# Rows of a 290-column operand at a pitch of 304 floats on 64-byte boundaries, and half of a normalization moved behind the second unit product

## The chip, the cores and the metric

The kernel runs as one program on one core of a Trainium2 chip. The metric is the device time of one execution in microseconds, a median over runs. Besides the runs, one execution was taken with the hardware profiler; every span, wait and duration below comes from that one.

## The reference

One step of one layer of a streaming encoder, for 512 prompt frames and 64 sample frames of width 2048, all in float32. The layer is an adaLN-modulated RMSNorm, an input projection, two recurrences (gated linear attention, 4 heads; gated delta rule, 8 heads), an output projection with a gated residual, then a second normalization and a convolutional feed-forward block of width 5632. The change lies in that second half:

```python
h = rmsnorm(x, norm2[l]) * (1 + sc2) + sh2
f, s_f = conv_ffn(h, ffn_s[l], w_up[l], ffn_conv_w[l], ffn_conv_b[l], w_down[l])
x = x + g2 * f

def conv_ffn(h, st, w_up, ffn_conv_w, ffn_conv_b, w_down):
    gate, val = jnp.split(h @ w_up, 2, axis=-1)
    gate_c, new_st = causal_dwconv(gate, st, ffn_conv_w)
    act = jax.nn.silu(gate_c + ffn_conv_b) * val
    return act @ w_down, new_st
```

## The kernel before

Activations lie transposed: features on the 128 partitions, frames along the row. The 576 frames are two halves of 288 columns (256 prompt, 32 sample frames). Every float32 product is made of three fp32r products: each operand is split into a rounded `hi` (ScalarE, `Copy`) and the rest `lo` (VectorE, subtraction), and TensorE adds `wh*hi`, `wh*lo` and `wl*hi` in PSUM. One matmul is 128 x 128 weights on 288 or 290 columns; TensorE issues a weight load and a matmul for each.

The stages, in order of time: the head with norm and modulation; the input projection (`gemm`, `mm6`, L534 and L536) with the recurrences' small work placed between its matmuls as jobs, and the rest of the modulation streamed through VectorE (L794); the first half of the output projection from 1100 us on; its second half with the second normalization begun tile by tile (`norm_tile`, `pair_early`, `pair_begin`); `up`, the feed-forward's first product; `down` and `final`.

A slot (`slot`) is an SBUF tile `[128, 2, w]`, w = 290 unless 288 is asked for. The residual stream's tiles `x1[m]` are slots (two rows: the two halves). So are the operands of `up`, where row 0 holds `hi` and row 1 `lo`. Two columns per half (256 and 257) carry the shift vectors through the product, which makes 290 of 288.

`up` multiplies by a 7-product scheme on 2 x 2 blocks (Strassen, in Winograd's form). For each of 44 column tiles t there are products c = 0 to 6 (`up_product`): 8 pairs j, three matmuls each (L1335 `wh, hi`; L1336 `wh, lo`; L1337 `wl, hi`), 24 of 290 columns. The right operands are the combinations B11, T1, T2, B21, T3, B22, T4, kept in slots for all t. For pairs 4 to 7 most of them are made during t = 0 (`pair_late`). `up_prep` splits the weights two products ahead. The sums gather in three PSUM banks of a pool of four (`bank`), x for c = 0 and 3, z for 1 and 5, y for 2, 4 and 6. `up_out` combines them.

The normalization's scale enters only behind the products, as a row `rb` (1/rms of each frame, on all partitions; first used in `up_out` for c = 3, L1355). `norm_tile` sums the squares into `sqa`, stores the tile to memory (`xd`, L1166) and scales it (L1168, L1169). `norm_end`, called behind the first product of t = 0, does the rest: ten small matmuls sum over the partitions (L1248), VectorE (L1250) and GpSimd (L1251) make rsqrt, VectorE spreads it to diagonals `dg` (L1253), two fp32 products with ones broadcast these (L1259, two passes each), ScalarE copies them over `sqa` (L1260), and GpSimd sets four entries to one (L1261).

A tile framework records the program and orders each engine's instructions by priorities and its own estimates of when they become ready; an engine then runs its instructions strictly in that order. Buffers are reused as soon as their last reader is done, so a buffer's size and place also decide what waits for what. DMAs are issued from SyncE's queue, a few from ScalarE's; none from GpSimd. 16 KB of every partition, from address 0, are set aside as scratch for dynamic DMA descriptors unless the program asks otherwise.

Of the kernel before, what the change touches and what calls it, by code (L numbers as in the profile page):

```python
# [8 lines left out]
F32 = mybir.dt.float32  # L9
# [7 lines left out]
P = 128  # L17
# [7 lines left out]


HZ, ZS = 290, 258
X_AT = (1, 2, 3, 4, 5)

AHEAD, JOB_AHEAD = 80, 80  # L30
# [67 lines left out]
class Kern:  # L98
# [530 lines left out]
    def head(self, pool):  # L629
# [16 lines left out]
        places = [f"h{c}{k}" for k in range(15, 4, -1) for c in "hl"]  # L646
        slot = lambda: self.hslot(places.pop(0), [P, 512])
        junk = slot()

        def x_block(b):  # L650
            n = P if b < 4 else TS
            xt = [slot() for _ in range(4)]
            for q in range(4):
                f = slice(q * 512, (q + 1) * 512)
                nc.sync.dma_start(xt[q][:n], i["x_prompt"][0, b * P:(b + 1) * P, f] if b < 4 else i["x_sample"][0, :, f])
            ms4 = pool.tile([P, 8], F32, tag="ms4", bufs=2, name=self.name("ms4"))
            for q in range(4):
                A.activation(junk[:n], xt[q][:n], AF.Square, scale=float(D) ** -0.5, accum_out=ms4[:n, q:q + 1])
            V.tensor_reduce(ms4[:n, 4:5], ms4[:n, 0:4], axis=mybir.AxisListType.X, op=ALU.add)
            self.rsqrt(ms4[:, 5:6], ms4[:, 4:5], 1, n)  # L660
            for q in range(4):
                V.tensor_scalar_mul(xt[q][:n], xt[q][:n], ms4[:n, 5:6])
            per = 4 if b < 4 else 8
            for k0 in range(0, KD, per):
                ps = self.pgt()[:, 0]
                for k in range(k0, k0 + per):
                    T.transpose(ps[:, (k - k0) * n:(k - k0 + 1) * n], xt[k // 4][:n, k % 4 * P:(k % 4 + 1) * P],
                                self.c["ident"][:n, :n])
                if b < 4:
                    A.activation(xT[:, k0:k0 + per, b // 2, (b % 2) * P:(b % 2 + 1) * P],  # L670
                                 ps.rearrange("p (k t) -> p k t", k=per), AF.Copy)
                else:
                    for h in range(2):
                        A.activation(xT[:, k0:k0 + per, h, HP:HT],
                                     ps.rearrange("p (k h t) -> p k h t", k=per, h=2)[:, :, h], AF.Copy)
# [5 lines left out]
        def modulation(g):  # L681
            for mi in (1, 0):
                ps = self.bank()
                c0 = mi * D + g * 512
                for k0 in range(0, KD, 4):
                    yield
                    raws = [hraw().rearrange("p (k n) -> p k n", k=2) for _ in range(2)]
                    for n, raw in enumerate(raws):
                        k1 = k0 + 2 * n
                        nc.sync.dma_start(raw, i["w_ada"][0, k1 * P:(k1 + 2) * P, c0:c0 + 512].rearrange("(k p) n -> p k n", p=P))  # L690

                    for k in (2, 3, 0, 1):
                        with self.tc.issue_after(last) if k == 0 else nullcontext():
                            T.matmul(ps[32 * k:32 * k + 32], cs[:, k0 + k], raws[k // 2][:, k % 2], start=(k0 == 0), stop=(k0 == KD - 4))  # L694
                        last = nc.cur_bb.bb.instructions[-1]
                rw = pool.tile([P, 512], F32, tag="rw", bufs=1, name=self.name("rw"))
                V.tensor_copy(rw, ps)
                pc = self.transpose4(rw.rearrange("p (b t) -> p b t", b=4))
                m = pool.tile([P, 4, 2], F32, tag="msum", bufs=2, name=self.name("msum"))
                V.tensor_reduce(m, pc.rearrange("p b (j q) -> p b q j", j=4)[:, :, 0:2], axis=mybir.AxisListType.X, op=ALU.add)  # L700
                self.put_mod(mi, 4 * g, m)
                for _ in vectors:
                    pass
            self.scale_mod(s1, 1, "norm1", 4 * g)

        for n, _ in enumerate(modulation(0)):
            if n in X_AT:
                x_block(X_AT.index(n))

# [432 lines left out]

    def slot(self, place, dt, w=HZ):
        pool, tag = place
        return pool.tile([P, 2, w], dt, tag=tag, name=self.name("slot"))

# [1 line left out]
    def norm_begin(self):  # L1150
        self.s2 = self.cp.tile([P, KD, 2], F32, name="s2")
        self.scale_mod(self.s2, 4, "norm2", 0, KD)
        self.sq = self.sp.tile([P, 2, HZ], F32, tag="sqa", bufs=1, name="sqa")
        self.combos = {}

    def norm_tile(self, m, first):
# [83 lines left out]
    def norm_end(self):  # L1240

        nc = self.nc
        V, A, T = nc.vector, nc.scalar, nc.tensor
        w = HZ // 5 * 2
        av = self.sq.rearrange("p h t -> p (h t)")
        ps = self.bank()
        for b in range(5):
            T.matmul(ps[:w, b:b + 1], av[:, b * w:(b + 1) * w], self.c["ones"][:, 0:1], start=True, stop=True)  # L1248
        rs = self.small(8)
        V.tensor_scalar(rs[:w, :5], ps[:w, :5], 1.0 / D, EPS, op0=ALU.mult, op1=ALU.add)  # L1250
        nc.gpsimd.tensor_tensor(rs[:w, :5], rs[:w, :5], self.mhalf[:w, :5], op=ALU.pow)  # L1251
        dg = self.ub.tile([P, 5, w], F32, tag="ca", name=self.name("dg"))
        V.tensor_tensor(dg[:w], self.c["ident"][:w, :w].unsqueeze(1).to_broadcast([w, 5, w]),  # L1253
                        rs[:w, :5].unsqueeze(2).to_broadcast([w, 5, w]), op=ALU.mult)
        rb = self.rb = self.sq
        dv = dg.rearrange("p b t -> p (b t)")
        for h in range(2):
            ps = self.bank()
            T.matmul(ps[:, :HZ], self.c["ones"][:w], dv[:w, h * HZ:(h + 1) * HZ], start=True, stop=True)  # L1259
            A.activation(rb[:, h], ps[:, :HZ], AF.Copy)  # L1260
        nc.gpsimd.memset(rb[:, :, HP:ZS], 1.0)  # L1261
# [138 lines left out]
    def up(self):  # L1400
        self.fs = self.cp.tile([P, 2, 2, NFF], F32, name="fs")
        self.cb = self.ub.tile([P, 2 * HZ], F32, tag="cb", name="cb")
        self.nc.gpsimd.tensor_copy(self.cb[:, 0:2], self.zero3[:, :2])
        self.up_state(0)
        self.t2s = {}
        ahead = 2
        steps = [(t, c) for t in range(NFF) for c in range(7)]
        for n, (t, c) in enumerate(steps):
            if t == 0:
                for l in ((1,), (2,), (3,), (4,), (5, 6), (), ())[c]:  # L1410
                    for j in range(N_EARLY, NPAIR):
                        self.pair_late(l, j)
            if n + ahead < len(steps):
                self.up_prep(*steps[n + ahead])
            self.up_product(t, c)
            if n == 0:
                self.norm_end()

            if t > 0 and c == 0:
                with self.tc.issue_after(self.split_of):  # L1420
                    self.up_conv(t - 1, self.ca)
                self.up_state(t)
            if t > 0 and c == 2:
                with self.tc.issue_after(self.split_of):
                    self.up_act(t - 1, self.v, self.ca)
            self.up_out(t, c)
        self.up_conv(t, self.ca)
        self.up_act(t, self.v, self.ca)
# [308 lines left out]
```

## Time and profile before

| | |
|---|---|
| median of 3 runs | 2957.4 us (2954.98 to 2959.34) |
| the profiled execution: span from first to last instruction | 2955.2 us |
| its own time beside the span | not recorded apart; the span stands 2.2 us under the median |
| mean granted TensorE clock | 0.982 |
| busy: TensorE, VectorE, ScalarE, GpSimd | 96%, 70%, 40%, 11% |
| unit products of `up` | 1364.7 to 2367.1 us |

Rows of groups read: line, engine, operation, output<-inputs, shapes, count, then busy time in us and the mean of one in ns. That mean is the life of one matmul in the pipeline; a new one starts about every 133 ns, so three are in flight. Rows of the timeline read: start, length, engine, line, and in brackets how long the engine was idle before and what released it. The granted clock (PEclk) is the share of full speed that the throttle lets TensorE have.

### The profile page before, as it was taken

The numbers are of one execution on the slowest core, as the hardware profiler recorded it, in microseconds if no ns is written. First come the engines' busy times: TensorE is split into PE (matmuls) and PEld (weight loads), VectorE is DVE, ScalarE is ACT, GpSimd is POOL, SyncE is SP. The second block draws the span as 40 slices with busy tenths as digits, with TensorE's granted clock in tenths as the row PEclk, the third lists the DMA queues.
The fourth block names the chain that finished last, engine by engine and source line by source line (L and its number), as shares of the span: only waits on it lengthen the run. The fifth ranks groups of instructions, "written<-read, shape, count | busy, mean of one in ns | idle before, by whom it ended". The sixth has DMA issues, their size and how long they took to land.

```text
span 2955.2 us, 52052 instructions
## 1 busy us (share of the span) xinstructions
PE 2836.7 (96%) x20964; PEld 2744.9 (93%) x20964; DVE 2055.8 (70%) x3299; ACT 1180.8 (40%) x2029; POOL 325.7 (11%) x513
## 2 busy tenths in 40 slices
PE   6998999999899999999999999999999999999998
PEld 3688988999889998999999999999999999999997
DVE  2357777776568877367888888888888855555455
ACT  4235444444454433255444444444444421212123
POOL 0004223332300000000111111111111100000000
PEclk8999999999999999999999999999999999999999
DMA  8864545444454547642433333333333463333221
GB/s 260 285 194 134 169 137 146 142 143 140 138 148 126 157 125 214 172 128 82 117 105 105 105 110 105 105 109 111 100 105 114 145 219 99 115 102 111 86 80 65
DMA packets 535444, 395.53 MB, mean 134 GB/s; under 512 B 59657, under 2 KB 465412, under 8 KB 535204
## 3 DMA queue, kind: packets, MB, share of 16 engines
q1 hardware_dynamic: 527860, 390.54, 44.2%
q8 instruction: 165, 2.70, 0.4%
q10 hardware_dynamic: 7344, 1.67, 0.3%
q14 instruction: 75, 0.61, 0.1%
HBM read 356.47 MB, written 35.67 MB: 133 GB/s over the span
## 4 chain that ended last, share of the span: by engine, by line
PE 80%; DVE 6%; DMA 5%; POOL 4%; ACT 3%; issue 2%; SPq 0%; ACTq 0%; POOLq 0%; DVEq 0%
PE g L534 25%; PE g L536 13%; PE bank L1336 11%; PE bank L1335 11%; PE bank L1337 11%; POOL m L1673 2%; DVE acc L794 2%; PE bank L153 1%; PE bank L694 1%; DMA xr<-in_w_ada_dram 1%; PE bank L425 1%; DVE wl L622 1%; ACT m L1658 1%; DVE m L1658 1%; DMA d<-m 1%
## 5 line engine op out<-in xcount | busy, mean ns | idle before, releaser
L1336 PE MATMUL bank<-slot,wh 128*128 128x290 f32 x2464 | 737.4, 299 | 0.0
L1335 PE MATMUL bank<-slot,wh 128*128 128x290 f32 x2464 | 733.3, 298 | 0.0
L1337 PE MATMUL bank<-slot,wl 128*128 128x290 f32 x2464 | 728.3, 296 | 0.0
L534 PE MATMUL g<-slot,wh 128*128 128x288 f32 x3168 | 552.8, 295 | 0.2 <-DVE slot L1105 0.2
L534 PE MATMUL g<-hh,wh 128*128 128x288 f32 x2048 | 474.2, 310 | 3.9 <-DVE conv_in L945 2.4
L621 ACT ACTIVATE wh<-raw 128x1024 fp32r<-128x1024 f32 x215 | 227.3, 1058 | 618.3 <-PE g L534 589.4
L1337 PEld LDWEIGHTS bank<-slot,wl 128*128 128x128 f32 x2464 | 470.6, 191 | 0.0
L1336 PEld LDWEIGHTS bank<-slot,wh 128*128 128x128 f32 x2464 | 468.8, 190 | 0.1
L534 PEld LDWEIGHTS g<-slot,wh 128*128 128x128 f32 x3168 | 464.5, 188 | 0.7 <-DVE slot L1105 0.5
L1335 PEld LDWEIGHTS bank<-slot,wh 128*128 128x128 f32 x2464 | 463.6, 188 | 0.1
L536 PE MATMUL g<-hh,wl 128*128 128x288 f32 x2048 | 450.1, 300 | 0.5 <-DVE wl L622 0.5
L534 PE MATMUL g<-hl,wh 128*128 128x288 f32 x2048 | 448.7, 299 | 0.7 <-DVE hl L1115 0.7
L1105 DVE SCALAR_TENSOR_TENSOR slot<-g,mod,slot 128x512 f32<-128x512 f32 (+1 forms) x448 | 201.6, 491 | 295.9 <-PE g L536 293.9
L794 DVE SCALAR_TENSOR_TENSOR acc<-xr,ct,acc 128x512 f32<-128x512 f32 x480 | 341.7, 750 | 28.5 <-DMA xr<-in_w_ada_dram 28.2
L534 PEld LDWEIGHTS g<-hh,wh 128*128 128x128 f32 x2048 | 331.3, 191 | 21.5 <-issue 14.2
L536 PE MATMUL g<-slot,wl 128*128 128x288 f32 x1584 | 342.7, 295 | 0.0
L536 PEld LDWEIGHTS g<-hh,wl 128*128 128x128 f32 x2048 | 333.2, 190 | 8.2 <-issue 6.7
L534 PEld LDWEIGHTS g<-hl,wh 128*128 128x128 f32 x2048 | 333.8, 190 | 5.7 <-issue 4.4
L622 DVE TENSOR_TENSOR wl<-raw,wh 128x1024 fp32r<-128x1024 f32 x215 | 262.3, 1220 | 51.0 <-ACT wh L621 48.8
L1282 ACT ACTIVATE wh<-raw 128x1024 fp32r<-128x1024 f32 x176 | 186.1, 1058 | 223.7 <-PE bank L1336 188.1
L536 PEld LDWEIGHTS g<-slot,wl 128*128 128x128 f32 x1584 | 256.1, 188 | 0.0
L1283 DVE TENSOR_TENSOR wl<-raw,wh 128x1024 fp32r<-128x1024 f32 x176 | 215.2, 1223 | 54.8 <-ACT wh L1282 54.8
(352 smaller groups left out, 3126.8 us busy)
## 6 DMA issues: line engine op xcount, KB each, us to landing
raw<-in_w_up_dram SPq DMA_DIRECT2D x176, 512.0 KB
xr<-in_w_ada_dram SPq DMA_DIRECT2D x128, 512.0 KB
raw<-in_w_in_dram SPq DMA_DIRECT2D x100, 512.0 KB
raw<-in_w_down_dram SPq DMA_DIRECT2D x88, 512.0 KB
hraw<-in_w_ada_dram SPq DMA_DIRECT2D x64, 512.0 KB
raw<-in_w_out_dram SPq DMA_DIRECT2D x32, 512.0 KB
slot<-actd SPq DMA_DIRECT2D x44, 288.0 KB
actd<-v SPq DMA_DIRECT2D x44, 256.0 KB
```

Of the source, the lines that this page charges most:

```text
L534: T.matmul(ps[:, h if bank is None else bank, :n], wh, x[:, h, :n], start=f, stop=False)
L536: T.matmul(ps[:, h if bank is None else bank, :n], wl, ah[:, h, :n], start=False, stop=stop)
L621: nc.scalar.activation(hi[:, :n_], raw[:, :n_], AF.Copy)
L622: nc.vector.tensor_tensor(lo[:, :n_], raw[:, :n_], hi[:, :n_].bitcast(F32), op=ALU.subtract)
L794: V.scalar_tensor_tensor(acc[s], w[:, k], col, acc[s], op0=ALU.mult, op1=ALU.add)
L1105: self.nc.vector.scalar_tensor_tensor(x1[:, :, z], ps[:, :, c], gain[:, q:q + 1], x1[:, :, z], op0=ALU.mult, op1=ALU.add)
L1282: self.nc.scalar.activation(hi, src, AF.Copy)
L1283: self.nc.vector.tensor_tensor(lo, src, hi.bitcast(F32), op=ALU.subtract)
L1335: T.matmul(ps, wh[:, j], hi, start=(c < 3 and j == 0), stop=False, skip_group_check=True)
L1336: T.matmul(ps, wh[:, j], lo, start=False, stop=False, skip_group_check=True)
L1337: T.matmul(ps, wl[:, j], hi, start=False, stop=(j == NPAIR - 1), skip_group_check=True)
L1658: return f(*a, **kw)
```

## The change

Three things change.

- `slot` allocates each row at a pitch of a multiple of 16 floats: 304 for 290, 288 for 288. The second row of a slot then starts 1216 bytes behind the first instead of 1160. A small `pad` tile is allocated and never written, and the descriptor scratch area is set to 512 bytes a partition. In the program as built, every row that TensorE streams from a slot or from the `hh` and `hl` tiles of the projections starts at a multiple of 64 bytes; before, they started at 0, 8, 32 or 40 modulo 64. The weights `wh` and `wl` start at 32 modulo 64 before and after. Tiles of 290 columns are no longer contiguous, so the stores to `xd` go as 256 pieces of 1160 bytes instead of 128 of 2320.
- `norm_end` becomes a generator that stops behind `dg`. Its second half (L1259 to L1261) is recorded behind the second unit product instead of the first.
- The order in which instructions stand on each engine is the same but for two stretches: from about 170 to 350 us, where the loads of the small constants and of the gates' vectors and the work that follows from them stand earlier, and the first products of `up`.

```diff
+ROW = 16
...
     def slot(self, place, dt, w=HZ):
         pool, tag = place
-        return pool.tile([P, 2, w], dt, tag=tag, name=self.name("slot"))
+        return pool.tile([P, 2, -(-w // ROW) * ROW], dt, tag=tag, name=self.name("slot"))[:, :, :w]
...
         self.sq = self.sp.tile([P, 2, HZ], F32, tag="sqa", bufs=1, name="sqa")
+        self.sp.tile([P, 8], F32, tag="pad", bufs=1, name="pad")
...
         rb = self.rb = self.sq
+        yield
         dv = dg.rearrange("p b t -> p (b t)")
         for h in range(2):
...
             self.up_product(t, c)
             if n == 0:
-                self.norm_end()
+                norm = self.norm_end()
+            if n < 2:
+                next(norm, None)
...
-    nc = bacc.Bacc("TRN2", target_bir_lowering=False, num_devices=1)
+    nc = bacc.Bacc("TRN2", target_bir_lowering=False, num_devices=1, dynamic_dma_scratch_size=512)
```

## The prediction

> **What bounds the kernel now.** I read the page first, then busy time by stage, then the groups of matmuls inside two stages. TensorE is busy 96% of the span, so the questions are where it still waits and what one matmul costs. By stage (columns: window, its length, then busy time and instructions of PE, weight loads, DVE, ACT, POOL; granted clock, DMA share, GB/s):
>
> ```profile
> PE 2836.7 (96%) x20964; PEld 2744.9 (93%) x20964; DVE 2055.8 (70%) x3299; ACT 1180.8 (40%) x2029; POOL 325.7 (11%) x513
> ...
> 230.00:260.00 30.00, 27.10 (x182) 26.41 (x180) 21.91 (x39) 20.03 (x44) 14.58 (x29) 0.89 0.60 174
> 260.00:300.00 40.00, 34.43 (x263) 33.03 (x263) 27.08 (x52) 13.16 (x44) 19.88 (x38) 0.94 0.41 113
> 300.00:350.00 50.00, 47.11 (x348) 45.15 (x347) 44.34 (x84) 27.58 (x73) 5.94 (x5) 0.95 0.62 184
> ...
> 1365.00:1380.00 15.00, 12.41 (x74) 11.74 (x73) 10.78 (x24) 8.53 (x18) 1.57 (x3) 0.77 0.38 105
> 1380.00:2371.00 991.00, 991.00 (x7363) 991.00 (x7362) 828.60 (x1024) 449.26 (x537) 106.61 (x131) 1.00 0.38 112
> 2371.00:2800.00 429.00, 429.00 (x3232) 429.00 (x3231) 228.54 (x375) 93.73 (x103) 0.00 (x0) 1.00 0.37 119
> ```
>
> From 1380 to 2800 us PE never stops, at full clock: there only a cheaper matmul can save time. In the unit products of `up` one matmul of 290 columns takes 991.00 / 7363 = 134.6 ns from start to start. The groups of that stage, and of the all-288 stretch 2380 to 2790 us, by form:
>
> ```profile
> L1336 PE MATMUL bank<-slot,wh 128*128 128x290 f32 x2445 | 731.0, 299 | 0.0
> L1335 PE MATMUL bank<-slot,wh 128*128 128x290 f32 x2444 | 726.3, 297 | 0.0
> L1337 PE MATMUL bank<-slot,wl 128*128 128x290 f32 x2445 | 722.1, 295 | 0.0
> ...
> L534 PE MATMUL g<-slot,wh 128*128 128x288 f32 x2059 | 357.5, 295 | 0.0
> L536 PE MATMUL g<-slot,wl 128*128 128x288 f32 x1030 | 220.4, 295 | 0.0
> ```
>
> The second stretch has 3089 matmuls in 410 us: 132.7 ns each. Scaled by columns, 290 should take 132.7 x 290 / 288 = 133.7. The unit products are 0.9 ns above that, and the row that stands out is L1336, which reads `lo`.
>
> **Term 1, the rows of `up`.** A slot holds `hi` and `lo` as two rows of 290 floats, 1160 bytes apart. In the program's addresses every `lo` row starts at 8 or 40 modulo 64 (2464 matmuls, L1336), while `hi` rows start at 0 or 32 (L1335, L1337). After the change all start at 0. Two sizes for what `lo` loses now: L1336's busy time less the mean of its neighbours is 731.0 - (726.3 + 722.1) / 2 = 6.8 us; and 0.94 ns over the scaled 288 times 7392 matmuls is 6.9 us. I take -6.8 us. The end on the other side is 0: L1336 is also always the second of its three, with the same weights as the one before. Against that, in `mm6` `lo` also follows `hi` under the same weights, there in aligned rows, and the groups of the projections show no such step:
>
> ```profile
> L534 PE MATMUL g<-hl,wh 128*128 128x288 f32 x1272 | 276.7, 298 | 0.0
> L536 PE MATMUL g<-hh,wl 128*128 128x288 f32 x1270 | 276.6, 298 | 0.0
> ```
>
> The Trainium skill, page "SBUF — State Buffer", Specifications (TRN2), gives SBUF lines of 16 bytes and a penalty for each new line. 1160 bytes touch 73 such lines from offset 0 and 73 from offset 8, so by counting lines this term would be 0; the 6.8 us of L1336 speak against that reading.
>
> **Term 2, the rows that move from 32 to 0.** I paired all 18,528 records of L1335 to L1337, L534 and L536 with the program's matmuls in order, and took start to start by address. In the 288-wide stages matmuls at 0 modulo 64 average 133.0 ns (76 tile-and-line groups), those at 32 average 132.2 (84 groups): aligned to 64 is 0.8 slower, with a standard error of 0.27. In `up` the `hi` rows give 133.8 against 133.5, not told apart. 5300 of the 288-wide matmuls stand at 32 and move to 0: at worst +0.8 x 5300 = +4.2 us; at best 0, if the difference is an accident of the tiles (one tile's mean lies anywhere from 130 to 136). I take half, +2.1, and +0.3 x 2464 = +0.7 for the `hi` rows of `up`. Alignment together: -6.8 + 2.1 + 0.7 = -4.0 us.
>
> **Term 3, the half of `norm_end` that moves.** The chain of waits around 1365 us, and the instructions there (start us, us, what):
>
> ```profile
> 1366.06 3.16 DMA xd<-slot
> 1369.33 0.34 POOL slot L1169
> 1369.68 1.14 POOL s L1251
> 1370.84 0.77 DVE dg L1253
> 1371.66 2.30 PE bank L1259 x4
> ```
>
> ```profile
> 1367.76 0.45 DVE L1187 TENSOR_TENSOR slot<-slot,slot 128x290 fp32r<-128x290 f32 x1
> 1367.97 1.09 PE L1248 MATMUL bank<-consts,sqa 128*116 128x1 f32 x10
> 1368.04 1.06 ACT L1282 ACTIVATE wh<-raw 128x1024 fp32r<-128x1024 f32 x1 [0.72 <-PE bank L1336]
> 1371.66 2.30 PE L1259 MATMUL bank<-dg,consts 116*128 116x290 f32 x4 [2.59 <-DVE dg L1253]
> 1372.26 0.45 DVE L1223 TENSOR_TENSOR v<-slot,slot 128x290 f32<-128x290 f32 x1
> 1373.03 0.41 ACT L1260 ACTIVATE sqa<-bank 128x290 f32<-128x290 f32 x1 [2.14 <-PE bank L1259]
> 1373.34 0.44 ACT L1186 ACTIVATE slot<-v 128x290 fp32r<-128x290 f32 x1
> 1373.34 0.86 PE L1335 MATMUL bank<-slot,wh 128*128 128x290 f32 x1
> ...
> 1388.14 0.30 PE L1335 MATMUL bank<-slot,wh 128*128 128x290 f32 x1
> ```
>
> PE waits 2.6 us for `dg`, whose POOL step stands behind the landing of the last `xd` store; then the clock is halved, so that unit product 1 (0 is the first) begins at 1373.34 and crawls. Product 5 begins at 1388.14. The clock by its own windows:
>
> ```profile
> 1366.80:1370.20 3.40, 2.27 (x21) 2.18 (x19) 2.31 (x6) 2.48 (x6) 0.87 (x2) 1.00 0.87 236
> 1370.20:1373.60 3.40, 1.94 (x5) 1.50 (x5) 2.76 (x6) 1.26 (x5) 0.60 (x1) 0.50 0.59 160
> 1373.60:1377.00 3.40, 3.40 (x15) 3.25 (x15) 2.57 (x6) 1.92 (x6) 0.10 (x1) 0.50 0.00 0
> ...
> 622.70:626.10 3.40, 1.99 (x15) 1.76 (x14) 3.33 (x4) 2.80 (x3) 0.00 (x0) 1.00 0.32 87
> 237.00:240.40 3.40, 1.33 (x11) 1.10 (x9) 2.41 (x7) 3.40 (x9) 1.45 (x1) 1.00 0.37 78
> 240.40:243.80 3.40, 2.57 (x9) 2.25 (x10) 3.40 (x8) 2.60 (x6) 0.00 (x0) 0.50 0.67 243
> ```
>
> A window with 1.33 us of work is followed by one at 0.50. One with 1.99 is not: the next stretch stays at full clock. In 1366.8 to 1370.2 stand 2.27 us, but 1.09 of these are the ten one-column matmuls of L1248, so 1.2 of real work.
>
> With the change product 1 follows L1248 directly at about 1369.0; its last T1 row is ready at 1368.2 (L1187), its weights before. It takes 24 x 134.6 ns = 3.2 us, to 1372.2, and covers `dg`, which ends at 1371.6 (cover 0.6 us). Real work in the first window rises to 2.4 us, so I expect the clock to hold. L1259's four passes, 1371.66 to 1373.34 at half clock, then take 0.84: to 1373.1. A new wait follows. In the changed program product 2 writes the PSUM bank that the first L1259 product used, so it waits for the ACT copy L1260. In ACT's changed order that copy stands behind the split of the last `v` (L1223 ends at 1372.7, split 0.43: 1373.1), another split (0.4) and a whole weight split of L1282's kind (1.06), which itself waits for product 1. So the copy ends at 1374.95 (behind it on ACT stand the splits of B22 and T4, wanted only from product 5 on); PE issues two matmuls of product 3 meanwhile and stands for some 1.5 us. Products 2, 3 (22 left) and 4 are 70 matmuls, 9.4 us: product 5 begins at 1384.4 instead of 1388.14, 3.7 us earlier. By DVE's changed order and the same durations product 5's `wl` is split at 1384.4, just when it is wanted: late next, if anything.
>
> The `xd` store is now 256 pieces of 1160 bytes instead of 128 of 2320. The nearest rows for the issue are these two:
>
> ```profile
> L1166 SPq DMA_DIRECT2D xd<-slot x16: 319/320/320, 1271.0 to 1366.1; - x16
> L1393 SPq DMA_DIRECT2D actd<-v x88: 524/571/1587, 1404.5 to 2372.2; - x88
> ```
>
> That is +0.25 us on SP, behind which only weight loads queue that have time; on the landing 0 to +1 us (a third of the 3.16), and it moves POOL, `dg` and ACT alike. I take 0.3. Term 3: -3.4 us; from -5.0 (no new wait) to -1.0 (landing +1, and one half-clock window of 3.4 us, costing 1.7).
>
> The Trainium skill, "TensorE: Matmul & The Clock Gate", Part 1, has the clock fall after an idle window of about 3.4 us; the trace agrees, the halved stretch being two such windows (1370.2 to 1377.0).
>
> **Term 4, what the freed 15.5 KB do.** The smaller scratch area moves the constants of `kp` off memory that the head still uses. In the changed order their load, now issued at 198.19 us, stands some 20 matmul groups earlier, and the gate matmuls and the first head's recurrence move up between the projections, until about 350 us. The work is the same. PE's waits from 170 to 350 us (total, times, longest):
>
> ```profile
> PE bank L292 <- DVE m L1658: 4.4, 1, 4.4
> PE g L534 <- DVE conv_in L945: 2.4, 1, 2.4
> PE bank L153 <- DVE kt L1658: 1.2, 1, 1.2
> ```
>
> The three windows from 230 lose 2.9 + 5.6 + 2.9 = 11.4 us. Both the chain and the matmuls that wait for it start earlier, so I take 0, between -4 and +4. The `pad` tile is never written. No DMA is issued from POOL, and the scratch area has no other user in the program: 0.
>
> **Sum.** -4.0 - 3.4 + 0 = -7.4 us on a span of 2955.2: 2947.8. The profiled execution's span stands 2.2 us under the median of the three runs (2957.4), taken to stay: 2950.0 us, -0.25%. About 0.2%, 5.9 us, can be told from no change; the runs shown spread over 4.4.
>
> **Rivals.** (1) *The rows bring nothing*: L1336 is slow for its place in the three, or what `lo` gains the rows moved from 32 to 0 give back (-6.8 + 4.2 + 0.7 = -1.9). Then only term 3 is left: 2952 to 2954. For it: the 0.8 ns between 0 and 32. Against: L1336's excess. Chance 0.22. The skill's TensorE page, Back-to-back issue gap, has a rule by columns and clock alone (290 / 2.4 + 2.5 = 123 ns wherever the row starts); this case's 134.6 does not agree. (2) *Rows at 0 are best for the weight loads too*, or the early waits shrink by 4: 2943 to 2946. No row speaks for it but the early waits. Chance 0.13. (3) *Slower*: the first head's matmuls, moved ahead in PE's own order, stand before their data. Place: 200 to 350 us. Price: a wait like L292's 4.4 us plus two half-clock windows behind it (6.8 us at half, 3.4 lost), 7.8 each. One undoes the gain (2957.8), two give 2965.6; it decides from the first full one. For it: PE waits in order, and this stretch already has such waits. Against: the chain's start moves as well. Chance 0.12. (4) My forecast: 0.53.
>
> **Numbers.** Predicted 2950.0; 2941 to 2958 takes in rivals 1 and 2, the bounds of term 3, and rival 3's first wait. Below 2951.5 (faster): 0.38 of my case's 0.53, rival 2's 0.13, and 0.04 of rival 1: 0.55. Above 2963.3 (slower): 0.08, rival 3 with two waits. Within: 0.37.
>
> **What would show it.** Right: the unit products from product 5 on shrink by about 6 us in all, with L1336's mean down to its neighbours'; no wait at L1259's successor, one of 1 to 2 us before product 2, ended by the ACT copy; clock at full speed through 1377. Wrong: L1336 still 3 ns above the others, the 288-wide stretch at over 133.5 ns, half clock after the norm products, or PE waits over 16 us between 230 and 350.

## The result and the profile after

The changed kernel takes 2965.2 us (median; 2961.7 to 2967.7), the kernel before 2956.2 us beside it: ratio 1.0033, 95% interval 1.0022 to 1.0043, or 9 us slower. A second set of runs gave 1.0041 (1.0029 to 1.0053). The profiled execution took 2961.7 us, 1.7 us more than its span of 2960.0.

TensorE is still the bound, and its matmuls have become dearer. The busy time of the page, then the windows that answer to those of before:

```profile
PE 2844.2 (96%) x20964; PEld 2749.4 (93%) x20964; DVE 2056.3 (69%) x3299; ACT 1175.1 (40%) x2026; POOL 324.2 (11%) x513
```

```profile
1380.00:2371.00 991.00, 990.87 (x7303) 990.64 (x7303) 823.74 (x1015) 446.06 (x534) 106.06 (x130) 1.00 0.38 110
2371.00:2800.00 429.00, 429.00 (x3220) 429.00 (x3219) 229.67 (x376) 95.45 (x106) 0.44 (x2) 1.00 0.37 121
```

In the same 991 us stand 7303 matmuls instead of 7363, in 429 us 3220 instead of 3232, at full clock and with next to no wait (0.13 us). The groups of the unit products show which passes lost (L1338 is `wh, hi`, L1339 `wh, lo`, L1340 `wl, hi`; L1335 to L1337 before):

```profile
L1338 PE MATMUL bank<-slot,wh 128*128 128x290 f32 x2435 | 727.9, 299 | 0.1
L1340 PE MATMUL bank<-slot,wl 128*128 128x290 f32 x2434 | 726.4, 298 | 0.0
L1339 PE MATMUL bank<-slot,wh 128*128 128x290 f32 x2434 | 723.2, 297 | 0.0
```

`lo` did get cheaper, 299 to 297 ns, and both `hi` passes dearer: 297 to 299 and 295 to 298. Then the waits from 1355 to 1400 us, the instructions there, and the clock:

```profile
PE bank L1250 <- DVE sqa L1167: 1.2, 1, 1.2
PE bank L1338 <- ACT sqa L1263: 0.2, 1, 0.2
```

```profile
1368.02 1.18 PE L1250 MATMUL bank<-consts,sqa 128*116 128x1 f32 x10 [1.22 <-DVE sqa L1167]
1369.06 0.38 PE L1338 MATMUL bank<-slot,wh 128*128 128x290 f32 x1
1370.15 0.96 ACT L1170 ACTIVATE slot<-slot,s 128x512 f32<-128x512 f32 x2 [1.69 <-DMA xd<-slot]
1373.89 1.14 PE L1262 MATMUL bank<-dg,consts 116*128 116x290 f32 x4
1375.07 0.69 ACT L1263 ACTIVATE sqa<-bank 128x290 f32<-128x290 f32 x2
```

```profile
1366.70:1370.10 3.40, 2.18 (x19) 2.08 (x19) 2.54 (x6) 1.76 (x3) 0.00 (x0) 1.00 0.68 174
1370.10:1373.52 3.42, 3.42 (x17) 3.42 (x16) 1.99 (x5) 2.46 (x7) 1.31 (x2) 0.50 0.79 220
1373.52:1376.93 3.41, 3.20 (x20) 2.73 (x20) 3.41 (x8) 2.58 (x6) 0.10 (x1) 1.00 0.00 0
```

The wait for `dg` is gone, as planned. A wait that the forecast didn't have stands in front of product 1: the ten small matmuls wait for the last `sqa`, and the clock still halves for one window.

The start of `up` scatters over 1363 to 1376 us between the profiles below, for both kinds of rows, so single spans are not compared; the times come from the runs, and from the profiles what repeats. The time from unit product 0 to 5 scatters too: the kernel after has 21.7 us in one profile, with 3.4 us at half clock behind product 0, and 27.0 in the other (e12, where 23 to 26 were expected), with 10.2 us at half clock; the kernel before has 6.8 us at half clock, and e1, e7 and e11 none. One profile's figure there is an example, not a price. Start to start of matmuls, in ns, worked out from the records' start times (a pass's figure runs from its matmul's start to the next one's; `up` from its third column tile on; "down" is the 288-wide ones behind `up`), with the time from unit product 0 to 5:

| kernel | up: wh hi, wh lo, wl hi | up | down | product 0 to 5, us | ratio to before |
|---|---|---|---|---|---|
| before | 134.6, 136.8, 132.6 | 134.64 | 132.82 | 23.4 | 1 |
| after | 137.0, 134.8, 135.3 | 135.67 | 133.25 | 21.7 | 1.0033 |
| after, second profile (e12) | 137.0, 134.8, 135.3 | 135.67 | 133.25 | 27.0 | 1.0041 |
| split alone (e1) | 134.6, 136.8, 132.6 | 134.64 | 132.80 | 19.7 | 0.9987 |
| rows alone (e2) | 137.0, 134.8, 135.3 | 135.67 | 133.25 | 27.8 | 1.0065 |
| after, rows at 32 (e3) | 134.8, 135.8, 134.6 | 135.08 | 133.24 | 24.4 | 1.0031 |
| after, rows at 8 (e4) | 134.3, 135.5, 134.8 | 134.84 | 133.24 | 25.5 | 1.0025 |
| scratch alone (e5) | 134.6, 136.8, 132.6 | 134.64 | 132.81 | 22.6 | 1.0006 |
| store in pieces alone (e6) | 134.6, 136.8, 132.6 | 134.64 | 132.82 | 23.6 | 1.0002 |
| after, whole stores (e7) | 137.0, 134.8, 135.3 | 135.67 | 133.25 | 20.2 | 1.0024 |
| after, pitch 1280 (e8) | 133.2, 133.4, 133.4 | 133.33 | 133.25 | 22.7 | 0.9988 |
| starts 60 and 112 (e9) | 129.2, 129.2, 134.9 | 131.11 | 130.22 | 25.5 | 0.9910 |
| starts 0 and 112 (e10) | 133.4, 133.2, 133.4 | 133.33 | 130.19 | 25.0 | 0.9945 |
| e9 with whole stores (e11) | 129.2, 135.0, 129.2 | 131.11 | 131.26 | 20.0 | 0.9885 |

### The profile page after: what moved, and what is told of

Same layout as the page of the kernel before. It is cut to its first block, busy times and chain, and to the rows that moved or that the text cites. A ratio compares the mean times of both kernels' runs of the same rounds, so it can differ in the third digit from the quotient of the medians.

```text
span 2960.0 us, 52030 instructions
## 1 busy us (share of the span) xinstructions
PE 2844.2 (96%) x20964; PEld 2749.4 (93%) x20964; DVE 2056.3 (69%) x3299; ACT 1175.1 (40%) x2026; POOL 324.2 (11%) x513
## 4 chain that ended last, share of the span: by engine, by line
PE 76%; DVE 8%; DMA 5%; POOL 4%; ACT 4%; issue 3%; SPq 0%; ACTq 0%; POOLq 0%; DVEq 0%
PE g L535 23%; PE g L537 12%; PE bank L1340 11%; PE bank L1338 11%; PE bank L1339 11%; POOL m L1678 3%; DVE acc L795 2%; DMA xd<-slot 1%; PE bank L695 1%; PE bank L154 1%; DMA xr<-in_w_ada_dram 1%; PE bank L426 1%; DVE wl L623 1%; ACT m L1663 1%; DMA d<-m 1%
## 5 line engine op out<-in xcount | busy, mean ns | idle before, releaser
L1338 PE MATMUL bank<-slot,wh 128*128 128x290 f32 x2464 | 737.6, 299 | 0.3 <-ACT sqa L1263 0.2
L1340 PE MATMUL bank<-slot,wl 128*128 128x290 f32 x2464 | 735.9, 299 | 0.0
L1339 PE MATMUL bank<-slot,wh 128*128 128x290 f32 x2464 | 732.9, 297 | 0.0
L1339 PEld LDWEIGHTS bank<-slot,wh 128*128 128x128 f32 x2464 | 470.2, 191 | 0.1
L1338 PEld LDWEIGHTS bank<-slot,wh 128*128 128x128 f32 x2464 | 467.6, 190 | 0.9 <-ACT sqa L1263 0.5
L1340 PEld LDWEIGHTS bank<-slot,wl 128*128 128x128 f32 x2464 | 467.6, 190 | 0.0
L1106 DVE SCALAR_TENSOR_TENSOR slot<-g,mod,slot 128x512 f32<-128x512 f32 (+1 forms) x448 | 201.8, 491 | 283.0 <-PE g L537 281.2
L1286 DVE TENSOR_TENSOR wl<-raw,wh 128x1024 fp32r<-128x1024 f32 x176 | 215.3, 1223 | 53.2 <-ACT wh L1285 53.2
```

The lines of the kernel that those rows point to most:

```text
L1106: self.nc.vector.scalar_tensor_tensor(x1[:, :, z], ps[:, :, c], gain[:, q:q + 1], x1[:, :, z], op0=ALU.mult, op1=ALU.add)
L1286: self.nc.vector.tensor_tensor(lo, src, hi.bitcast(F32), op=ALU.subtract)
L1338: T.matmul(ps, wh[:, j], hi, start=(c < 3 and j == 0), stop=False, skip_group_check=True)
L1339: T.matmul(ps, wh[:, j], lo, start=False, stop=False, skip_group_check=True)
L1340: T.matmul(ps, wl[:, j], hi, start=False, stop=(j == NPAIR - 1), skip_group_check=True)
```

## The experiments

**The parts alone.** e1 puts only the generator into the kernel before, e2 takes only the generator out of the kernel after, e5 gives the kernel before only the small scratch area.

```
e1  before + "yield" in norm_end, next(norm, None) for n < 2
e2  after with  self.norm_end()  in one piece behind product 0
e5  before + dynamic_dma_scratch_size=512
```

> Kernel before with the split of norm_end alone: rows, pitch and scratch area as before. Theory 1 (the split gains what the trace of after shows around the first unit products, and all of the loss lies in the rows): product 5 begins 1.7 us earlier after the start of up than before (23.4 us behind product 0 becomes 21.7), the 24 matmuls of a product stay at 134.6 ns from start to start, and the time is 1.5 to 3.5 us under the kernel before. Rival (the split itself brings the loss, through another order of the instructions of up): matmuls at 135.7 ns and the time 5 us or more above the kernel before.

> Kernel after without the split: rows at a pitch of 304, pad and scratch area of 512 bytes. Theory 1 (the rows cost): 135.7 ns a matmul in the unit products, so 7 to 8 us in up, 1.6 us in down, and about 10 to 12 us above the kernel before. Rival (the split brings the loss): 134.6 ns and within 2 us of the kernel before, or below it.

> Kernel before with the scratch area of 512 bytes alone: the load of the small constants and the early work move as in the kernel after, rows stay at a pitch of 1160 and at their old starts modulo 64. Forecast's Term 4: 0, between -4 and +4 us. Theory C of the pitch: the starts modulo 1024 move by 512, so a matmul in up may change by a few tenths of a ns; theories A and B: it stays at 134.6 ns.

Measured: e1 0.9987 (0.9978 to 0.9996), 3.8 us faster; e2 1.0065 (1.0052 to 1.0077), 19 us slower, more than the 10 to 12 expected; e5 1.0006 (0.9997 to 1.0015). So the split gains, the rows cost, and the early reordering is not told from nothing. The loss of e2 in `up` and `down` is 1.03 x 7392 + 0.43 x 4224 = 9.4 us; its first unit products, in the one profile, add 4.4. The other 5 us stand in no row that was read.

**Another start, same pitch.** Is it the start modulo 64, or the distance of 1216?

```
e3  after, slot(): [:, :, (8 if w == HZ else 0):][:, :, :w]
e4  after, slot(): [:, :, (2 if w == HZ else 0):][:, :, :w]
```

> Kernel after, but the slots of 290 begin at column 8 of their rows: every row that TensorE streams in up starts at 32 modulo 64, as the weights do, instead of 0; the distance between hi and lo stays 1216 bytes. Theory A (the distance of 1216 bytes, a multiple of 64, is what makes a matmul slower): 135.7 ns stay, time within 2 us of the kernel after. Theory B (rows at 0 beside weights at 32 are the slow pair): 132.5 to 134 ns, 12 to 23 us under the kernel after. Theory C (no rule by the start modulo 64 at all; the mean over the sequence of addresses lies anywhere from 134 to 136.5): a value in that span that follows neither, with the three lines out of step from those of the kernel after.

> Kernel after, but the slots of 290 begin at column 2 of their rows: all rows start at 8 modulo 64, where the second row of every pair stood in the kernel before. Forecast's reading (a start at 8 is what made L1336 slow before, by 2.8 ns): all three lines slow, 136 to 137 ns, 2 to 10 us above the kernel after. Theory A (the distance counts, not the start): 135.7 ns, within 2 us of the kernel after. Theory C (no rule by the start): anywhere from 134 to 136.5 ns, all three lines moved.

Measured: up 135.08 and 134.84 ns; times 1.0031 (1.0019 to 1.0042) and 1.0025 (1.0014 to 1.0037). Rows at 8, which the forecast took for the slow class, are the fastest of the three at this pitch from start to start (the three times lie within each other's intervals); rows at 32 like the weights are no remedy. Theories A and B fall in these forms, and so does the forecast's own reading; both values lie in theory C's span.

**The matmul by itself.** Zeros, one PSUM bank, nothing else running, one execution; groups of 96, means over the last 71.

> The matmul by itself: all of the layer is left out and zeros are written. Groups of 96 matmuls of 128 x 128 weights on 290 columns (a few groups on other widths), all in one PSUM bank, back to back. Series A: one row, at 20 starts modulo 1024, weights at 480. B: row at 0, weights at 16 starts modulo 1024. C: two rows in turn at 11 distances. D: two weights in turn at 5 distances. F: widths 256 to 304. E: the real threes (wh hi, wh lo, wl hi), eight pairs, in ten layouts, each in three orders of the threes. Forecast's reading (a row at 8 modulo 64 costs 2.8 ns against 0): A differs by that between 8, 40 and 0, 32, 64. Theory B (start against the weights' start): A and B differ by the difference of the two starts. Theory A (distance of hi and lo): C at 1216 stands 1 ns or more over 1160. Theory C (a state that the last few reads leave, no rule by one address): A and B flat within 1 ns at about 133 to 135, the layouts of E spread over 134 to 137, and in E the layout of 1216 over that of 1160.

One row over and over, weights at 480: at 0, 8 and 40 modulo 64 the same 133.3 ns, so the class of L1336 costs nothing by itself. But rows at 64 take 135.0, at 96 136.0, at 128 136.6, at 384 (128 modulo 256) 136.7, at 256, 512 and 768 133.3. With the row at 0 and the weights moved instead: 133.3 at 0, 136.6 at 96, 136.0 at 128 and at 384. Two rows in turn: 133.3 at distances 1024, 1280 and 2048, 135.5 at 1216. So series A and B are not flat, as theory C had them: the start counts even with one row over and over. The real threes, each group of 96 as a window (columns as in the windows above): pitch 1160, then 1216, then 1280:

```profile
830.40:843.23 12.83, 12.83 (x98) 12.83 (x97) 0.00 (x0) 0.00 (x0) 0.00 (x0) 1.00 0.00 1
869.09:882.18 13.09, 13.09 (x98) 13.09 (x97) 0.00 (x0) 0.00 (x0) 0.00 (x0) 1.00 0.00 1
1063.10:1075.90 12.80, 12.80 (x98) 12.80 (x97) 0.00 (x0) 0.00 (x0) 0.00 (x0) 1.00 0.01 1
```

The count takes in two or three of the neighbouring groups; over 96 they are 133.6, 136.4 and 133.3 ns. By passes, pitch 1160 gives 133.3, 136.6, 131.1, and 1216 gives 139.5, 135.0, 135.7: the slow pass of the kernel before is `lo`, that of the kernel after `hi` with `wh`, as in the table. The pattern comes from the addresses and their order, without VectorE, ScalarE or a DMA. Its size does not carry over: by itself the pitch of 1216 stands 2.8 ns over 1160, in the kernel 1.03. And the pitch alone does not set it: the same rows at 1216, taken as `wh, hi`, `wl, hi`, `wh, lo`, need 133.3 ns over the last 71 instead of 136.7. That order was not tried in the kernel.

**All distances a multiple of 256.** The change is `ROW = 64` in the kernel after: pitch 1280, every slot at a multiple of 256.

> Kernel after with ROW = 64 instead of 16: rows of slots at a pitch of 1280 bytes (320 floats), every slot at a multiple of 256 bytes, so all rows of up at 0 modulo 256, the weights as before at 224 modulo 256. Theory C as the matmul by itself made it precise (reads whose starts differ by a multiple of 256 keep one steady relation to the weight loads, 133.33 ns; other distances wander between 126 and 148 ns and average 133.3 to 136.7): every matmul of up takes 133.3 ns, all three lines alike, 2.34 x 7392 = 17.3 us less in up than the kernel after; the 288-wide ones of down 133.3 ns as now; the time 7 to 10 us under the kernel before. Rival (the larger pitch alone does not decide, since the passes of the real kernel share the memory with VectorE, ScalarE and the DMAs): 134 to 136 ns, within 8 us of the kernel after.

```profile
1400.00:2330.00 930.00, 930.00 (x6977) 930.00 (x6976) 781.28 (x957) 421.14 (x499) 101.87 (x124) 1.00 0.38 109
2380.00:2760.00 380.00, 380.00 (x2852) 380.00 (x2851) 198.77 (x326) 80.44 (x88) 0.00 (x0) 1.00 0.36 111
```

930.00 / 6977 = 133.3 ns, on all three lines alike. 0.9988 (0.9978 to 0.9998): 3.4 us under the kernel before, less than the 7 to 10 expected, with the dearer `down` (+1.8) and the wait for `sqa` still in it. The expectation left out the projections: from 350 us on their matmuls now take 133.3 ns from start to start instead of 132.8, some 2 us over 4900 of them.

**Which start.** With one start for all rows, modulo 256:

> The matmul by itself again, all of the layer left out and zeros written: the real threes on eight pairs with rows at a pitch of 1280 and steps of 2560, so that all rows have one start modulo 256; this start goes from 0 to 252 in steps of 4 (weights at 224 modulo 256), then down again in steps of 16, then the weights' start goes from 0 to 240 with rows at 0; then sixes as in down on 288 columns at pitches 1280 and 1152. If one relation of row start to weight start decides (theory B in its modulo-256 form): each start has its own value, the same on the way up and down, the same for equal differences of row and weights, and some starts lie under 133.3 ns. If a multiple of 256 as the distance is enough: all 133.3 ns. If the state left by earlier reads decides: up and down differ.

Rows at 0, 60 and 176 (the second time on the way down) on 290 columns, and at 112 on 288:

```profile
86.02:98.82 12.80, 12.80 (x98) 12.80 (x97) 0.00 (x0) 0.00 (x0) 0.00 (x0) 1.00 0.00 1
279.34:291.93 12.59, 12.59 (x99) 12.59 (x97) 0.00 (x0) 0.00 (x0) 0.00 (x0) 1.00 0.00 0
652.80:666.22 13.42, 13.42 (x99) 13.42 (x97) 0.00 (x0) 0.00 (x0) 0.00 (x0) 1.00 0.00 1
962.17:975.60 13.43, 13.43 (x99) 13.43 (x97) 0.00 (x0) 0.00 (x0) 0.00 (x0) 1.00 0.00 1
1503.85:1516.34 12.49, 12.49 (x98) 12.49 (x97) 0.00 (x0) 0.00 (x0) 0.00 (x0) 1.00 0.00 1
```

In steady state that is 133.3, 131.1, 140.0, 140.0 and 130.0 ns. Over 64 starts the values lie from 131.1 to 140.0. On the way down 12 of 16 starts gave what they had given going up; 32, 80, 208 and 224 gave another value (80: 133.3, then 131.1). So the starts decide in the main, and some starts have two steady patterns, which the reads before seem to choose between. Modulo 256 is a rule with exceptions: rows at 256, 512 and 768 took what 0 took, and 384 what 128 took, but weights at 64 and 320 gave 133.4 and 136.0. One expectation failed: the difference of row and weights does not decide. Rows at 176 beside weights at 224 take 140.0 ns; weights at 48 beside rows at 0, the same difference, take 134.0. Both theories had a part of it.

**The better starts in the real kernel.**

```
e9   e8, slot(): [:, :, (15 if w == HZ else 28):][:, :, :w]
e10  e8, slot(): [:, :, (0 if w == HZ else 28):][:, :, :w]
```

> As the kernel with rows at a pitch of 1280, but the slots of 290 begin at column 15 (60 modulo 256) and the slots of 288 at column 28 (112 modulo 256). In the matmul by itself these starts gave 131.14 ns (290, threes; seen once, going up) and 130.01 ns (288, sixes), against 133.33 at 0. If the start relative to the weights' decides in the real kernel as well: 131.1 ns in up (16 us less than at 0), 130.0 ns in down (13 us less), the time 25 to 33 us under the kernel before. If the steady relation at such starts is only one of several, into which the run can fall by the reads just before (as 32, 80, 208 and 224 gave two values each): 133.3 to 136 ns in up or down, and the time anywhere from 20 us under to 20 us over the kernel before, with the pitch changing between products within one run.

> As the kernel with rows at a pitch of 1280, the slots of 290 at 0 modulo 256 as there, only the slots of 288 at 112 modulo 256. up: 133.33 ns. down: 130.0 ns if the start decides (13 us less, the time 15 to 18 us under the kernel before), 133.3 or more if it does not (2 to 6 us under).

```profile
1400.00:2330.00 930.00, 930.00 (x7094) 929.85 (x7093) 795.63 (x975) 428.63 (x508) 104.84 (x128) 1.00 0.38 110
2380.00:2760.00 380.00, 380.00 (x2926) 380.00 (x2925) 206.23 (x337) 84.89 (x93) 0.00 (x0) 1.00 0.35 109
```

These rows are of e9: 131.1 ns in `up`, 129.9 in `down` (130.0 by the records, since a window's count takes in the matmuls at its edges), as the matmul by itself had said; e10 has 133.33 and 130.19. Times: 0.9910 (0.9891 to 0.9930), 29 us under the kernel before, and 0.9945 (0.9928 to 0.9961), 17 us. The starts of the rows are shown as the cause, and they work in both directions.

**The stores.** Where does the wait for `sqa` come from?

```
e6   before, xd tiles [2, P, HZ]: same tile in SBUF, 256 pieces of 1160 bytes
e7   after, the whole padded tile stored and loaded: 128 pieces of 2432 bytes
e11  e9, the whole tile: 128 pieces of 2560 bytes
e12  after, unchanged
```

> Kernel before, with the stores to xd alone changed: its memory holds the two rows apart, so each store goes as 256 pieces of 1160 bytes as in the kernel after, from the contiguous tile; rows in SBUF, order and scratch as before. Theory 1 (the pieces make each store land later, which ScalarE's scaling in place waits for): ScalarE's idle time before it rises from 21 to about 32 us over the 16 tiles, a new wait of 1 to 3 us of the ten small matmuls for sqa stands behind the first unit product, and the time is 3 to 8 us above the kernel before. Rival (the pieces cost the 0.3 us of the forecast, and the later landing in the kernel after comes from reading rows at a pitch of 1216): ScalarE's wait stays at 21 to 23 us and the time within 1.5 us of the kernel before.

> Kernel after, but each store to xd takes the whole padded tile, 128 pieces of 2432 bytes (16 small memsets of the pad are added on GpSimd in the head of the projection), and the loads back likewise. Theory 1 (the pieces cost): ScalarE's wait for xd falls from 32 to about 22 us, no wait for sqa, and the time 2 to 7 us under the kernel after, so 2 to 7 us above the kernel before. Rival (the pieces are free): as the kernel after, 8 to 9 us above the kernel before.

> As the kernel with starts at 60 and 112 modulo 256, but each store to xd takes the whole tile in 128 pieces of 2560 bytes (32 small memsets of the pad on GpSimd; loads back likewise). If the pieces, through ScalarE's wait for xd, delay sqa and bring the wait behind the first unit product: ScalarE's wait falls from 33.6 to 17 to 23 us, the wait for sqa of 2.9 us goes, product 0 to product 5 takes 19.5 to 21 us instead of 25.5, and the time is 3 to 5 us less, 30 to 34 us under the kernel before. Rival (the wait for sqa comes from the changed order on VectorE): it stays at 2 us or more, and 26 to 30 us under the kernel before.

> The kernel after once more, unchanged, for a second profile and more runs. If the profiled execution of it that is at hand stands for it: 135.67 ns in up, a wait of the ten small matmuls for sqa of 1.2 us, product 0 to product 5 in 21.7 us. If the wait scatters as in the kernels with other starts (2.4 to 2.9 us): 23 to 26 us. The time 6 to 12 us above the kernel before.

ScalarE's scaling of a tile in place waits until its store has read it. The groups of that line from 1100 to 1376 us (the last figures are its idle time and who ended it), before, after, e6, e7 and e11:

```profile
L1168 ACT ACTIVATE slot<-slot,s 128x512 f32<-128x512 f32 (+1 forms) x32 | 15.4, 529 | 21.2 <-DMA xd<-slot 21.2
```

```profile
L1170 ACT ACTIVATE slot<-slot,s 128x512 f32<-128x512 f32 (+1 forms) x32 | 15.4, 529 | 32.4 <-DMA xd<-slot 32.4
```

```profile
L1168 ACT ACTIVATE slot<-slot,s 128x512 f32<-128x512 f32 (+1 forms) x32 | 15.4, 529 | 28.6 <-DMA xd<-slot 28.5
```

```profile
L1173 ACT ACTIVATE slot<-slot,s 128x512 f32<-128x512 f32 (+1 forms) x30 | 14.4, 527 | 17.2 <-DMA xd<-slot 17.2
```

```profile
L1175 ACT ACTIVATE slot<-slot,s 128x512 f32<-128x512 f32 (+1 forms) x32 | 15.4, 529 | 17.4 <-DMA xd<-slot 17.4
```

Against the kernel before, ScalarE's wait is (28.6 - 21.2) / 16 = 0.5 us a tile longer in e6 and 0.7 in the kernel after; with whole stores of the padded tile it is no longer than before. All eight profiles with padded rows stored in pieces have a wait of L1250 for `sqa`, of 1.2 to 2.9 us; with whole stores it is 0 (e7, e1) or 0.3 (e11). PE's waits from 1355 to 1400 us in e12 and e11:

```profile
PE bank L1250 <- DVE sqa L1167: 2.9, 1, 2.9
PE bank L1338 <- ACT slot L1188: 1.1, 1, 1.1
```

```profile
PE bank L1343 <- ACT sqa L1268: 1.5, 1, 1.5
PE bank L1255 <- DVE sqa L1172: 0.3, 1, 0.3
PE bank L1343 <- DVE v L1366: 0.2, 1, 0.2
```

With the split, product 0 to 5 takes 24.5 us in the mean of the seven profiles with pieces, 20.0 in the three without. In time: e7 1.0024 (1.0015 to 1.0033), a little under both sets of the kernel after; e11 0.9885 (0.9870 to 0.9900), 34 us under the kernel before, the fastest kernel here, 7 us under e9 where 3 to 5 were expected, though its `down` is 1.04 x 4224 = 4.4 us dearer. Both intervals touch those of the same kernel with pieces, so the waits tell the stores apart and the times do not. Against the expectation, e6 cost nothing (1.0002, 0.9993 to 1.0010): from a contiguous tile in the kernel before the pieces are hidden, with a wait for `sqa` of only 0.2 us. So the pieces alone are not enough; it takes the padded rows. The traces show the difference at the store itself, with the same number and size of pieces in e6 and in the kernel after: SyncE takes 0.32 us to issue one before, 0.36 in e6, 0.52 in the kernel after and 0.32 in e7, and from the start of that issue to the end of the last piece it is 1.7, 1.9, 2.3 and 1.7 us (medians of 16). So e6's rival was in part right. Why pieces out of a padded tile are dearer is not settled.

## Why the prediction was wrong

**What bounds the kernel** was right: matmuls from 1380 us on, one at a time.

**Terms 1 and 2, the rows, failed.** The step that failed is "every `lo` row starts at 8 or 40 modulo 64", taken as the reason why L1336 was slow, with 0 as the end on the other side. Measured per pass: `lo` -2.0 ns x 2464 = -4.9 us, but `hi` with `wh` +2.4 x 2464 = +5.9 and `hi` with `wl` +2.7 x 2464 = +6.7: +7.7 us where Terms 1 and 2 together had -6.1 for `up`. In series A a row at 8 costs what a row at 0 does. L1336 was slow because of the sequence of starts around it: the slow pass moved to another line, and the three passes together went from 403.9 to 407.0 ns. The 288-wide part was near: +1.8 us in `down` and nothing in the projections (132.95 and 132.97 ns), forecast +2.1. The Trainium skill, "TensorE: Matmul & The Clock Gate", Back-to-back issue gap, says that the spacing in a stream is set by the weight load and the matmul together; series B agrees in kind (moving only the weights, 133.3 to 136.6 ns), while its formula for an isolated matmul, which the forecast held against this stream, has no place for a start.

**Term 3, the split, had the right mechanism and the wrong store.** Where the stores are whole it is worth 23.4 - 20.0 = 3.4 us (2.6 against e5's 22.6, also without the split), the forecast's -3.4, and e1's time agrees (-3.8; -6.5 to -1.2). The step that failed is the one on the `xd` store, "on the landing 0 to +1 us", taken at 0.3 and followed from the last store alone. That store kept to its bounds (3.94 us against 3.16), and the issue was near the forecast (+0.20 us for +0.25). But every one of the 16 stores lands later. The chain of the kernel after shows how an earlier store reaches `sqa` by way of ScalarE's scaling and VectorE's queue:

```profile
1359.08 3.17 DMA xd<-slot
...
1362.34 0.96 ACT slot L1170 x2
1363.30 0.35 ACT slot L1188
...
1363.67 0.71 DVE slot L1189 x2
...
1365.25 0.86 DVE slot L1106 x2
...
1366.13 3.94 DMA xd<-slot
```

On VectorE a weight split (L1286) and then the last addition to `sqa` (L1167, at 1367.21) stand behind that L1106. The wait for it comes before product 1, where PE idles long enough that a halved window follows: 24.5 us in the mean, +1.1 against the one profile of before. The forecast looked only at what stands behind the last store. The wait for ScalarE's copy of 1.5 us was 0.2 here, presumably since product 1 itself ran at half clock; in e7 and e11, at full clock, it is 1.4 and 1.5. The clock rule read from the trace held: 2.18 us of PE work, about 1.2 of it in one-column matmuls, and the next window at 0.50.

**Term 4** was right: e5 gives 0 within 0.15%, though the waits changed place (the longest one before 350 us is now 5.4 us).

**Sum:** +7.7 + 1.8 + 1.1 = +10.6 us, measured 9.0 (6.5 to 12.7). The parts add up within the interval, but the +1.1 rests on profiles that scatter by 5 us. No rival had this case: rival 3's price for two waits, 2965.6 us, lies beside the measured 2965.2 by luck, since its early waits cost nothing (e5). The slower case was sought in the early waits, and that rows could cost was bounded at +4.2 + 0.7, from two averages that mixed many relations of rows and weights.

## What to carry to other kernels

A mean per line over mixed addresses is no price for a start: before rows are moved, time the real sequence of row and weight starts by itself, since a few groups of 96 matmuls showed which passes are slow at pitches 1160 and 1216, though not by how much, and foretold the 131.1 and 130.0 ns of e9 to within 0.2 (though e11 shows that a start can have two values). In this kernel it paid to give all streamed rows one start modulo 256 and to choose that start by such a run. When a tile is padded, look at whether its stores still go in one piece a partition, and follow a store to everything that writes its source in place.

## What the runs showed that was not expected

- With one row start modulo 256, a 290-column fp32r matmul takes a steady mean from 131.1 to 140.0 ns, by the start of the rows and of the weights; some starts have two such means (80: 133.3 and 131.1). Around that mean single matmuls spread over 12 ns at some starts and over 1 ns at start 0. With mixed starts they lie between 126 and 148.
- By width, at start 0 with the weights at 480: 256 columns 116.6 ns, 280 127.7, 288, 290 and 292 all 133.3, 296 136.7, 304 140.0.
- A state persists: in e9 and e11 the same starts gave 129.9 and 380.00 / 2900 = 131.0 ns in `down` from 2380 to 2760 us, and in `up` the slow pass of 135.0 ns was `wl, hi` in one and `wh, lo` in the other, from the second tile on. In e11 it stays so to the end. In e9 one matmul of the last tile, at 2341.31 us, takes 207 ns, and from the next one on the slow pass is `wh, lo` there too: the pattern changed at a gap in the stream, seen this once.

```profile
L1340 PE MATMUL bank<-slot,wl 128*128 128x290 f32 x2365 | 699.8, 296 | 0.0
L1338 PE MATMUL bank<-slot,wh 128*128 128x290 f32 x2365 | 686.0, 290 | 0.0
L1339 PE MATMUL bank<-slot,wh 128*128 128x290 f32 x2364 | 685.6, 290 | 0.0
```

```profile
L1344 PE MATMUL bank<-slot,wh 128*128 128x290 f32 x2365 | 700.0, 296 | 0.0
L1343 PE MATMUL bank<-slot,wh 128*128 128x290 f32 x2366 | 686.1, 290 | 0.0
L1345 PE MATMUL bank<-slot,wl 128*128 128x290 f32 x2365 | 685.9, 290 | 0.0
```

What in the memory has the period of 256 bytes, and what picks one of two steady patterns at the start, stays open.
